# 1388 one-pass products of many widths and operand places, behind the last TensorE operation of a hybrid decoder step

## The chip, the cores and the metric

The kernel runs on one core of a Trainium2 chip, and its time is the device time in microseconds. A profile of one execution gives busy times, waits and the order of the instructions on each engine; its span reaches from the first to the last instruction, and the execution's own time is a little longer.

## The reference, cut to what matters

One inference step of one decoder layer, for a prompt of 256 tokens and 8 single new tokens, 264 columns in all. All data are float32.

```python
def swiglu(x, wg, wu, wd):
    return (jax.nn.silu(x @ wg) * (x @ wu)) @ wd

def trunk_layer(x, attend, shift0, wkv0, lp):
    ...
    x = x + FFN_RES * swiglu(rmsnorm(x, n1), f1g, f1u, f1d)
    h = rmsnorm(x, nm)
    proj = h @ w_in
    ...
    mixed = jnp.concatenate([o_att, o_rwkv.astype(o_att.dtype)], axis=-1)
    x = x + mixed @ w_out
    x = x + FFN_RES * swiglu(rmsnorm(x, n2), f2g, f2u, f2d)
    return x, k_buf, v_buf, S, shift

y_prompt = rmsnorm(xp, final_norm)
y_sample = rmsnorm(xs, final_norm)
```

The model width is 2048 and the FFN width 5504. The attention and the RWKV recurrence between the two FFNs do not touch the change.

## The kernel before, in words

Activations lie transposed: 128 features on the partitions, the 264 tokens as columns. A weight matrix is worked through in blocks of 128 by 128. So that a float32 product can run in TensorE's one-pass format (`F32R` in the code), every operand is split into a rounded part `hi` and the rest `lo`, and three one-pass products stand for one exact product: `hi` with `xh`, `hi` with `xl`, and `lo` with `xh` (`gemm`, lines 136 to 150, through the helper `mm`, line 74). Each call of `mm` on one-pass operands leaves one weight load and one product in the trace; a call on plain float32 operands leaves two of each.

`chunk` (line 125) brings four weight blocks, 512 columns, at a time: SyncE's queue loads `raw`, ScalarE makes `hi`, VectorE makes `lo`. There are four buffers each of `hi` and `lo`. `gemm` sums into a PSUM tile of tag `acc` (three buffers); everything smaller writes tiles of tag `m` (five buffers, `mp`, line 122).

`ffn` (line 227) goes through the 43 FFN blocks in six parts (`PARTS`): the gate and up products of a part, the activation, and then for each of the 16 output blocks `o` the down product of this part, whose result is added to `xr[o]` (line 296). In the last part there are seven blocks, so that each output block has a chunk of four and one of three.

At the end `second_ffn` (line 960) normalises: the sums of squares go through TensorE into `sm`; three products into `hot`, which nobody reads, follow; ScalarE and VectorE make the reciprocal root `rt`; TensorE broadcasts it to all partitions twice, into `rp` for VectorE and into `again`, which ScalarE copies to `rb` for GpSimd. Nine multiplications (lines 998 to 1001) on VectorE and GpSimd scale the stored `ys`, and each is followed by its output DMA on SyncE's or ScalarE's queue. At the start of the kernel `NWARM` = 11 products of `ones` with itself write a tile `warm` that nobody reads either (lines 162 to 164).

A scheduler in the compiler orders each engine's instructions by their place in the program and by when it thinks that their operands are ready; the program states no order by hand around the changed place.

The memory map of the program puts rows of moving operands 1280 bytes apart (`ROW` = 320, line 110) and weight blocks 512 bytes apart.

Of the kernel before, what the change touches and what calls it, by code (L numbers as in the profile page):

```python
# [13 lines left out]
P = 128  # L14
NP = 256
NB = 8
T = NP + NB
# [10 lines left out]
CH, NRAW, NHL = 4, 6, 4  # L28
# [19 lines left out]
def body(tc, I, O):  # L48
    nc = tc.nc
    V, A, G, TE, SP = nc.vector, nc.scalar, nc.gpsimd, nc.tensor, nc.sync  # L50
    cnt = [0]
    big = [None]

    def uid(s):
        cnt[0] += 1
        return f"{s}{cnt[0]}"
# [4 lines left out]
    def stt(out, a, s, b, op0, op1):  # L61
        return V.scalar_tensor_tensor(out=out, in0=a, scalar=s, in1=b, op0=op0, op1=op1)  # L62
# [11 lines left out]
    def mm(out, lhsT, rhs, start=True, stop=True, **k):  # L74
        return TE.matmul(out, lhsT, rhs, start=start, stop=stop, **k)  # L75
# [24 lines left out]
    with ExitStack() as ctx:  # L100
# [21 lines left out]
        def mp():  # L122
            return pp.tile([P, 512], F32, tag="m", bufs=NM, name=uid("m"))
# [12 lines left out]
        def gemm(ps, src, xs, step=None, rng=None, ahead=True, ready=None):  # L136
            n = len(xs)
            for k0 in range(0, n, CH):
                k1 = min(n, k0 + CH)
                if rng and k0 not in rng:  # L140
                    continue
                hi, lo = ready or chunk(src[:, k0 * P:k1 * P], k1 - k0, V, ahead)
                for k in range(k0, k1):
                    xh, xl = xs[k]
                    c = slice((k - k0) * P, (k - k0 + 1) * P)
                    mm(ps[:, :T], hi[:, c], xh, k == 0, False)
                    mm(ps[:, :T], hi[:, c], xl, False, False)
                    big[0] = mm(ps[:, :T], lo[:, c], xh, False, k == n - 1)
                if step:
                    step()  # L150
# [15 lines left out]
        def vc(i):  # L166
            return vec[:, i:i + 1]
# [59 lines left out]
        def ffn(nrm, xr, gu, dn, nxt, load, begin=None, side=None, ready=None):  # L227
            rstd = None
            f0 = 0
            for pi, nf in enumerate(PARTS):  # L230
                hs = hblock(nf)
                late = []
                if begin:
                    early(pi)
                first = pi == 0
                if first:
                    banks = [acc() for _ in range(NACC)] + [mp() for _ in range(NM)]
                    n0 = len(banks) // 2
                    for k in range(len(nrm.xs), CH):
                        at = load(k)  # L240
                    for k0 in range(0, KD, CH):
                        if begin and k0 + CH < KD:
                            begin(k0 // CH + 1)
                        xs = nrm.xs + [None] * (KD - len(nrm.xs))
                        for i, ps in enumerate(banks):
                            with tc.issue_after(at.ins) if begin and k0 == 0 < i else nullcontext():
                                gemm(ps, gu[i // 2, i % 2], xs, rng=(k0,), ahead=False, ready=ready)
                            ready = None
                            if i >= len(banks) - CH and k0 + CH < KD:
                                load(k0 + CH + i - len(banks) + CH)  # L250
                    for f in range(n0):
                        raw = [tmp(), tmp()]
                        V.tensor_copy(raw[0], banks[2 * f][:, :T])
                        A.copy(raw[1], banks[2 * f + 1][:, :T])
                        late.append((f, *raw))
                for f in range(f0 + n0 if first else f0, f0 + nf):
                    pgu = [acc(), acc()]
                    if first and f == n0:
                        sq = iter(range(KD))

                        def step():
                            for k in [x for _, x in zip(range(2), sq)]:
                                nrm.square(xr[k], k % 2, True)
                    else:
                        step = None
                    if begin and pi and copies:
                        copy_one()
                    if side and pi:
                        next(side, None)
                    for ps, w in zip(pgu, (gu[f, 0], gu[f, 1])):  # L270
                        gemm(ps, w, nrm.xs, step)
                    last = f == f0 + nf - 1
                    if rstd is None:
                        rstd = nrm.rstd(tmp())
                    late.append((f, *(x[:, :T] for x in pgu)))
                    now = [late.pop()]
                    for _ in range(len(late) if last else min(len(late), 2 if first and f == n0 + 1 else 1)):
                        now.append(late.pop(0))
                    for j, pg, pu in now:
                        E = V if last else G  # L280
                        g = tmp()
                        tt(V, g, pg, rstd, ALU.mult)
                        s = tmp()
                        act(s, g, AF.Silu)
                        u = tmp()
                        tt(V, u, pu, rstd, ALU.mult)
                        tt(E, u, u, s, ALU.mult)
                        hi, lo = hs[j - f0]
                        A.copy(hi, u)
                        tt(E, lo, u, hi.bitcast(F32), ALU.subtract)  # L290
                if pi == len(PARTS) - 1:
                    nrm.xs = None
                for o in range(KD):
                    ps = acc()
                    gemm(ps, dn[o, :, f0 * P:(f0 + nf) * P], hs)
                    stt(xr[o], ps[:, :T], 0.5, xr[o], ALU.mult, ALU.add)
                    if pi == len(PARTS) - 1:
                        nxt(o)
                f0 += nf

        def first_ffn(n2):
            def load(k0):
# [657 lines left out]
        def second_ffn(n3, xr, XR):  # L960
            fin = Norm(VGF, most=3)

            def load(k):
                if k >= CH:
                    n3.split(xr[k], True)

            with tc.tile_pool(name="f2", bufs=1) as fp:
                cur[0] = (fp, NH)
                ys = [fp.tile([P, 4, T], F32, tag="y", bufs=4, name=uid("y")) for _ in range(4)]
                rt = fp.tile([88, 48], F32, name="rt")  # L970
                sq = fp.tile([P, NQ, T], F32, name="sq")
                n3.sq = fin.sq = [sq[:, j] for j in range(NQ)]

                def nxt(o):
                    fin.square(xr[o])
                    if o == 0:
                        act(rt[:, 7:8], fin.sums[0][0][0:88, 0:1], AF.Sqrt)
                    act(ys[o // 4][:, o % 4], xr[o], AF.Copy, scale=vc(VGF + o))

                side = dec_state(fp, XR)  # L980
                ffn(n3, xr, I["gu2"], I["dn2"], nxt, load, None, side)
                assert next(side, side) is side
                p = fin.sums[0]
                sm, rp, hot = mp(), mp(), mp()
                for i, q in enumerate(p):
                    for j in range(3):
                        mm(sm[0:88, j:j + 1], q[:, j * 88:j * 88 + 88], ones[:, 0:1], i + j == 0, i == 1, skip_group_check=True)
                for _ in range(3):
                    mm(hot[:, :P], ones, p[1][:, :P])
                act(rt[:, 0:3], sm[0:88, 0:3], AF.Sqrt, scale=1.0 / D, bias=eps[0:88, 0:1])  # L990
                V.reciprocal(rt[:, 0:3], rt[:, 0:3])
                for j in range(3):
                    mm(rp[:, j * 88:j * 88 + 88], bc(rt[:, j:j + 1], (88, P)), C[0:88, CID:CID + 88])
                rb, again = tmp(), mp()
                for j in range(3):
                    mm(again[:, j * 88:j * 88 + 88], bc(rt[:, j:j + 1], (88, P)), C[0:88, CID:CID + 88])
                A.copy(rb, again[:, :T])
                for i, (e, o, n) in enumerate(((V, 0, 1), (V, 1, 1), (V, 2, 2), (V, 4, 4), (G, 8, 1), (V, 9, 2), (G, 11, 1), (V, 12, 3), (G, 15, 1))):
                    y = ys[o // 4][:, o % 4:o % 4 + n]
                    r = rb if e is G else rp[:, :T]  # L1000
                    tt(e, y, y, bc(r.unsqueeze(1), (P, n, T)), ALU.mult)
                    (SP, A)[i % 2].dma_start(O["yT"][:, o:o + n, :], y)
# [111 lines left out]
```

## Time and profile before

| what | value |
|---|---|
| median of 2 runs | 1960.09 us (1959.72 to 1960.45) |
| the profiled execution's own time | 1958.83 us |
| its span | 1957.0 us |
| mean granted TensorE clock | 0.998 of full speed |
| PE busy | 1940.1 us, 17011 records |
| PEld busy (weight loads) | 1922.1 us, 17011 records |
| DVE busy | 1313.1 us |
| ACT busy | 1036.4 us |
| POOL busy | 264.1 us |
| HBM | 346.67 MB read, 9.69 MB written |

PE stands for TensorE's products, PEld for its weight loads, DVE for VectorE, ACT for ScalarE, POOL for GpSimd, SP for SyncE; a q behind the name is the engine's sequencer. In lines that group instructions, the shapes stand before the count (x...), then busy time in us and mean duration of one in ns, then the idle time before them. Durations of products overlap, so that the pace of TensorE is read from the starts and not from the durations. In timeline lines the first number is the start in us, the second the time from the first start to the last end of the merged instructions. Since `mm` is one line of code (L75), the products are told apart by their tiles: out<-moving operand,weights.

### The profile page before, as it was taken

To read this page: it belongs to the slowest core of one execution; us is meant where nothing else is said; L and a number is where in the kernel's file an instruction comes from. 1 tells how busy PE (TensorE), PEld (TensorE's weight loads), DVE (VectorE), ACT (ScalarE), POOL (GpSimd) and SP (SyncE) were. 2 spreads that over 40 slices of the span, in tenths; PEclk is the share of its full clock that TensorE was granted. 3 is DMA by queue.
4 is the path that set the end of the run, shared out by engine and by line. 5 is a ranking of instruction groups with operands and counts; after the bars stand their busy time and mean duration, and the time that the engine had idled before them with its cause. 6 is when DMAs were issued, how large, how long until landed. Compare 5 with 4: busy or idle time off the path is not lost.

```text
span 1957.0 us, 45229 instructions
## 1 busy us (share of the span) xinstructions
PE 1940.1 (99%) x17011; PEld 1922.1 (98%) x17011; DVE 1313.1 (67%) x2591; ACT 1036.4 (53%) x2069; POOL 264.1 (13%) x382
## 2 busy tenths in 40 slices
PE   9999999999999999999999999999999999999998
PEld 9999999999999999999889999999999999999998
DVE  5865555655556567799988766766666666666665
ACT  5644444444444456665556755654444444444445
POOL 0401001010010122232210000210101001010012
PEclk9999999999999999999999999999999999999999
DMA  7666666666656567555455455566666666666654
GB/s 241 178 194 194 186 194 196 184 189 178 188 183 185 184 194 230 165 162 153 136 151 167 137 157 185 176 187 188 191 189 193 188 194 191 191 195 183 195 182 148
DMA packets 218875, 357.26 MB, mean 183 GB/s; under 512 B 33552, under 2 KB 72352, under 8 KB 218656
## 3 DMA queue, kind: packets, MB, share of 16 engines
q1 hardware_dynamic: 212144, 345.76, 59.4%
q10 hardware_dynamic: 6512, 8.61, 1.4%
q8 instruction: 133, 2.18, 0.4%
q14 instruction: 86, 0.70, 0.1%
HBM read 346.67 MB, written 9.69 MB: 182 GB/s over the span
## 4 chain that ended last, share of the span: by engine, by line
PE 95%; DVE 3%; DMA 1%; issue 1%; ACT 1%; SPq 0%; DVEq 0%; POOL 0%; ACTq 0%
PE acc L75 87%; PE m L75 7%; DVE lo L59 1%; DVE Xt L59 0%; DVE st L59 0%; DMA Xt<-sa 0%; DMA x<-in_x 0%; DMA raw<-in_win 0%; DVE y L59 0%; SPq L564 0%; DVE gm L59 0%; ACT t L69 0%; DMA sa<-gm 0%; PE m L782 0%; ACT BT L521 0%
## 5 line engine op out<-in xcount | busy, mean ns | idle before, releaser
L59 DVE TENSOR_TENSOR lo<-raw,hi 128x512 fp32r<-128x512 f32 (+1 forms) x1288 | 874.5, 683 | 511.0 <-ACT hi L132 489.8
L132 ACT CAST hi<-raw 128x512 fp32r<-128x512 f32 (+1 forms) x1288 | 777.0, 606 | 822.0 <-PE acc L75 741.5
L75 PE MATMUL acc<-x,hi 128*128 128x264 f32 x5034 | 932.7, 286 | 2.2 <-DVE o L62 1.2
L75 PEld LDWEIGHTS acc<-x,hi 128*128 128x128 f32 x5034 | 781.4, 189 | 5.8 <-ACT hi L132 2.4
L75 PE MATMUL acc<-x,lo 128*128 128x264 f32 x2517 | 719.8, 286 | 0.5 <-DVE lo L59 0.5
L75 PE MATMUL acc<-h,hi 128*128 128x264 f32 x2752 | 495.0, 284 | 0.0
L75 PEld LDWEIGHTS acc<-x,lo 128*128 128x128 f32 x2517 | 475.5, 189 | 2.9 <-DVE lo L59 1.3
L75 PEld LDWEIGHTS acc<-h,hi 128*128 128x128 f32 x2752 | 424.4, 189 | 0.0
L75 PE MATMUL acc<-h,lo 128*128 128x264 f32 x1376 | 387.8, 284 | 0.0
L75 PEld LDWEIGHTS acc<-h,lo 128*128 128x128 f32 x1376 | 259.2, 189 | 0.0
L59 POOL TENSOR_TENSOR t<-t,t 128x264 f32<-128x264 f32 x74 | 80.3, 1085 | 1095.9 <-DVE t L59 949.7
L75 PE MATMUL acc<-y,hi 128*128 128x264 f32 x648 | 122.7, 284 | 0.0
L75 PE MATMUL acc<-o,hi 128*128 128x264 f32 x648 | 120.1, 284 | 0.0
L75 PE MATMUL acc<-kv,hi 128*128 128x264 f32 x582 | 109.2, 284 | 0.0
L75 PEld LDWEIGHTS acc<-y,hi 128*128 128x128 f32 x648 | 101.2, 189 | 0.1
L75 PEld LDWEIGHTS acc<-o,hi 128*128 128x128 f32 x648 | 100.1, 189 | 0.0
L62 DVE SCALAR_TENSOR_TENSOR x<-acc,x 128x264 f32<-128x264 f32 x192 | 81.2, 427 | 24.5 <-PE acc L75 23.6
L75 PE MATMUL acc<-y,lo 128*128 128x264 f32 x324 | 92.0, 284 | 0.0
L75 PE MATMUL acc<-o,lo 128*128 128x264 f32 x324 | 92.0, 284 | 0.0
L75 PEld LDWEIGHTS acc<-kv,hi 128*128 128x128 f32 x582 | 90.0, 189 | 0.0
L59 DVE TENSOR_TENSOR t<-acc,t 128x264 f32<-128x264 f32 x156 | 67.4, 432 | 32.8 <-PE acc L75 32.8
L75 PE MATMUL acc<-kv,lo 128*128 128x264 f32 x291 | 82.7, 284 | 0.0
(280 smaller groups left out, 1534.9 us busy)
## 6 DMA issues: line engine op xcount, KB each, us to landing
raw<-in_gu SPq DMA_DIRECT2D x688, 256.0 KB, 3.4
raw<-in_dn SPq DMA_DIRECT2D x224, 256.0 KB, 2.9
raw<-in_win SPq DMA_DIRECT2D x152, 256.0 KB, 3.4
raw<-in_dn SPq DMA_DIRECT2D x160, 192.0 KB, 2.7
raw<-in_wout SPq DMA_DIRECT2D x64, 256.0 KB, 3.3
xsp<-x ACTq DMA_DIRECT2D x16, 132.0 KB, 3.6
x<-xsp SPq DMA_DIRECT2D x16, 132.0 KB, 4.0
ld<-in_sT SPq DMA_DIRECT2D x16, 128.0 KB, 3.7
```

The lines of the kernel that those rows point to most:

```text
L59: return e.tensor_tensor(out=out, in0=a, in1=b, op=op)
L62: return V.scalar_tensor_tensor(out=out, in0=a, scalar=s, in1=b, op0=op0, op1=op1)
L75: return TE.matmul(out, lhsT, rhs, start=start, stop=stop, **k)
L132: A.copy(hi[:, :w], raw[:, :w])
```

## The change

`gemm` now notes the `hi` and `lo` of the latest chunk of four blocks in a list `wl`, and `ffn` copies that list to `held` after each down product. A new function `wide` is called once, behind the copy of `again` to `rb` and ahead of the nine final multiplications. It allocates one more PSUM tile of tag `m` and multiplies the held `hi` (as weights) with the held `lo` (as moving operand), always into the same tile, each product a group by itself; nobody reads the tile. First come 14 widths of the moving operand, six products each, then 4 widths of the weights, six each, then 256 pairs of starting places, five each: 84 + 24 + 1280 = 1388 products. A step of 4 elements is 16 bytes. All other code stays.

```diff
+    wl = []
...
                 hi, lo = ready or chunk(src[:, k0 * P:k1 * P], k1 - k0, V, ahead)
+                if k1 - k0 == CH:
+                    wl[:] = [hi, lo]
...
                     stt(xr[o], ps[:, :T], 0.5, xr[o], ALU.mult, ALU.add)
+                    held[:] = wl
...
+        held = []
+
+        def wide(w, x):
+            ps = mp()
+            for n in (264, 256, 248, 240, 272, 280, 288, 296, 304, 320, 384, 448, 512, 264):
+                for i in range(6):
+                    mm(ps[:, :n], w[:, 0:P], x[:, 0:n])
+            for m in (32, 64, 96, 128):
+                for i in range(6):
+                    mm(ps[:m, :T], w[:, 0:m], x[:, 0:T])
+            for c in range(0, 64, 4):
+                for d in range(0, 64, 4):
+                    for i in range(5):
+                        mm(ps[:, :T], w[:, c:c + P], x[:, d:d + T])
...
                 A.copy(rb, again[:, :T])
+                wide(*held)
                 for i, (e, o, n) in enumerate(...):
```

## The prediction

> **What bounds the kernel now.** I read the page first: busy shares, the granted clock, the chain that ended last.
>
> ```profile
> span 1957.0 us, 45229 instructions
> PE 1940.1 (99%) x17011; PEld 1922.1 (98%) x17011; DVE 1313.1 (67%) x2591; ACT 1036.4 (53%) x2069; POOL 264.1 (13%) x382
> ...
> PEclk9999999999999999999999999999999999999999
> ...
> PE 95%; DVE 3%; DMA 1%; issue 1%; ACT 1%; SPq 0%; DVEq 0%; POOL 0%; ACTq 0%
> ```
>
> TensorE is the bound: 95% of the chain that ended last is PE, at a clock that the throttle never cut in any slice. So there is no room inside the kernel for 1388 more products; what matters is what one costs and what already stands behind the last of TensorE's work. For the first, the chain over the last stretch, in order of time (start, us, what):
>
> ```profile
> 1929.97 15.13 PE acc L75 x126
> ...
> 1946.13 2.10 PE m L75 x18
> 1948.23 0.02 issue
> 1948.26 0.43 DVE y L59
> 1948.68 0.34 DVEq L1110
> 1949.03 3.28 DVE y L59 x4
> ```
>
> 126 one-pass products of 264 columns take 15.13 us on the chain: 120.1 ns from start to start, with weights loaded anew for each. That pace is the price to carry over. The duration that the groups give is longer, because products overlap in the pipeline:
>
> ```profile
> L75 PE MATMUL acc<-h,hi 128*128 128x264 f32 x2752 | 495.0, 284 | 0.0
> L75 PE MATMUL acc<-y,hi 128*128 128x264 f32 x648 | 122.7, 284 | 0.0
> L75 PE MATMUL acc<-kv,hi 128*128 128x264 f32 x582 | 109.2, 284 | 0.0
> L75 PE MATMUL m<-ones 128*128 128x128 f32 x22 | 4.3, 378 | 1.0 <-POOL eps L159 1.0
> L75 PE MATMUL m<-o,ones 128*128 128x264 f32 x6 | 1.7, 384 | 0.0
> L75 PE MATMUL m<-C,rt 88*128 88x88 f32 x12 | 1.5, 276 | 0.0
> ```
>
> A lone product is in flight for 284 ns, but the next starts after 120; 284 counts once, for the very last. For the second question, the timeline of PE at the end and one stretch of full-precision products for comparison:
>
> ```profile
> 1944.81 0.28 PE L75 MATMUL acc<-h,lo 128*128 128x264 f32 x1
> 1944.93 0.56 PE L75 MATMUL m<-ones,sq 128*88 128x1 f32 x6
> 1946.13 0.63 PE L75 MATMUL m<-ones,sq 128*88 128x1 f32 x6 [0.65 <-ACT sq L69]
> 1946.62 0.91 PE L75 MATMUL m<-sq,ones 128*128 128x128 f32 x6
> 1947.38 1.51 PE L75 MATMUL m<-C,rt 88*128 88x88 f32 x12
> ```
>
> ```profile
> 64.75 1.05 PE L75 MATMUL m<-o,ones 128*128 128x264 f32 x4
> ```
>
> The last weight multiplication of the second FFN starts at 1944.81; then come the sums of squares, the three products on `hot`, and the two broadcasts of the scale (`rp` and `again`, 12 records). PE is through at 1947.38 + 1.51 = 1948.89. A float32 product leaves two records, a one-pass product one. In the run of four float32 records of 264 columns the pace is (1.05 - 0.384) / 3 = 0.222 us a record.
>
> After PE's end 8 us of the span are left: DVE's, ScalarE's and GpSimd's final multiplications, the output DMAs, and the closing drain:
>
> ```profile
> L1110 SPq EVENT_SEMAPHORE  x7: 17/28/3839, 1951.9 to 1957.0; - x7
> L1110 POOLq EVENT_SEMAPHORE  x4: 17/17/17, 1956.4 to 1956.9; - x4
> L1110 PEldq DRAIN  x2: 13/785/1557, 1947.4 to 1956.7; - x2
> ```
>
> SP waits 3.839 us for the outputs' landing; from 1956.4 GpSimd collects the engines, and the span ends at 1957.0. Only these 0.6 us must follow whichever engine is last.
>
> **The change, part by part.** Nothing is removed. The two list assignments run while the program is built and issue no instruction. Keeping `hi` and `lo` of the last four-block chunk alive costs nothing: no later chunk asks for a buffer. The target takes a fifth buffer of tag `m`, beside `sm`, `rp`, `hot` and `again`, and there are five. No product reads what another engine has yet to make, so no wait is added, and no DMA is issued. Products into one bank one after the other are what the 126 of the chain are too.
>
> *Where they begin.* The last record of `m<-C,rt` starts 0.276 before its end, at 1948.61. The pace of that run is (1.51 - 0.276) / 11 = 0.112 us, so the first new product starts near 1948.73. If the compiler's scheduler instead lets a few into PE's wait of 0.65 us for `sq`, the end comes up to 0.65 us sooner; the sum of TensorE's work stays.
>
> *Column part: 84 products.* The fourteen widths add up to 4376, times six 26,256 columns. By 120 ns for 264, 0.4545 ns a column: 11.9 us. Bounds: a constant 120 ns for widths up to 264 and in proportion above gives 12.1; half of the float32 record's 222 ns, 0.4205 ns a column, gives 11.0. The trace has no one-pass product narrower than 264. If the 12 with 240 and 248 columns lost the one-pass price and cost two float32 records (404 and 417 ns), they would add 3.5 us. I take 11.9, since the row of one-pass products is nearest.
>
> *Narrow weights: 24 products of 264 columns with 32, 64, 96 and 128 weight columns.* At 120 ns: 2.9 us. Nearest bounds for the 18 narrow ones: 222 ns a piece adds 1.8 us; below, weights of 32 columns that run beside each other could save at most their 2.2 us. I take 2.9.
>
> *Places: 16 x 16 x 5 = 1280 products of 264 columns.* At 120 ns: 153.6 us. This is the term that decides, and it is the one the trace shows least. In the program's memory map all 14,976 one-pass products of before have the moving operand at byte 96 modulo 256 and the weights at byte 160 modulo 256: one of the 256 combinations that the loops visit. There `y`, `kv` and `h`, tiles far apart, have the same 284 ns a product in the groups. Bounds for another place: below, 112 ns (the pace of `m<-C,rt`, where 88 columns leave only the load of 128 weight columns to bind; half of the float32 record, 111, says the same); above, 222 ns, the pace of a float32 record of the same width, which streams two cycles a column. I take 120 everywhere, as the only row of the same operation.
>
> A rule stands against this price. The Trainium skill, page "TensorE: Matmul & The Clock Gate", section "Back-to-back issue gap", gives columns / 2.4 plus 2.5 ns for a warm stream, 112.5 ns for 264 columns. By it the whole addition would be an estimated 157.9 us in place of 168.4. The trace's 120 ns over 126 products disagrees with it, at a full clock, so the measurement decides.
>
> *Sum.* 11.9 + 2.9 + 153.6 = 168.4 us. The last product ends at 1948.73 + 168.4 - 0.12 + 0.284 = 2117.3. All that followed PE before (final multiplications from 1948.26, output DMAs, SP's wait) now runs beside the new products, which are thirty times as long; were that cover gone, it would cost up to 8 us. Then 0.6 us of closing: span 2117.9. The profiled execution took 1958.83 us, 1.83 more than its span: 2119.7. The median of the two timed runs, 1960.09, lies 1.26 above that execution, so the forecast for the median is 2121.0.
>
> **The rivals.**
>
> *Some places are dear.* If weights and moving operand are read from the same part of memory in the same step, the array waits, and some of the 256 combinations pace slower than 120. For it: 120 ns lies about 8 ns over the two rows that say 111 and 112, so something already holds a one-pass product back, and the trace has only one combination. Against it: the duration is the same to the nanosecond for tiles all over memory. Price: every nanosecond of the mean over places is 1.28 us; one place in five at 222 ns adds 26 us, 2147; a third of them adds 44, 2165; all of them 131, 2252. The Trainium skill says, on the TensorE page named above, section "Part 2: What happens when you issue a matmul", that weights and moving operand come through two independent read ports and loading does not take bandwidth from a running product; by that rule no place would be dear. No trace here shows two places.
>
> *Most places are cheaper.* If the 8 ns over 112 belong to the one combination of before, the 1304 products of 264 columns save 8 ns each, 10.4 us, and the columns up to 0.9: about 2110. For it: the two rows just named. Against it: the pace after the last one-pass product, before a load of only 88 weight columns, is still 1944.93 - 1944.81 = 0.12 us, so the 120 look like the product's own time.
>
> *The products are dropped.* Nobody reads the target, and a compiler may strike out work that nobody reads; then the time stays at 1960, not slower. It decides once fewer than 39 / 0.12 = 327 of the 1388 are left (2% of 1960 is 39 us, about what a measurement of this kernel can tell from no change). Against it: the eleven warm-up products at the start are read by nobody either, and their 22 records stand in the trace (`m<-ones`); so do the six of `hot`.
>
> **How the numbers follow.** Flat at 120 ns, 2121 with 2112 to 2128 as its own range (narrow widths, narrow weights and a nanosecond or two of the places): 0.58. Dear places: 0.27. Cheaper places: 0.12. Dropped: 0.03. The range from 2108 to 2165 takes in the flat case, nearly all of the cheap one and half of the dear one. Slower by over 2%: 0.97, all cases but the last; within 2%: 0.02; faster by over 2%: 0.01, for what I have not seen.
>
> **What would show it.** PE's records rise by 1388 to about 18,400, one for each product; the 1280 stand at starts 0.120 us apart. The chain ends in PE, not in DVE's `y`; the output DMAs have landed near 1956 as before, and the closing after PE's drain takes under 1 us. The granted clock stays full to the end. In the column part the widths show whether pace follows columns or stands at a floor, and whether 240 and 248 jump to 400 ns. I would be wrong if the pace changes from place to place (the place term), if the first new product starts before 1946 or well after 1949, or if the final multiplications wait behind the new products.

## The result, and the profile after

The changed kernel takes 2126.2 us (median of two runs, 2126.15 to 2126.26) against 1960.09: ratio 1.0848, 95% interval 1.0801 to 1.0894. The forecast was 2121.0 within 2108 to 2165. Its profiled execution took 2126.26 us. The kernel before took from 1957.24 to 1962.77 us in sixteen of its seventeen executions beside the second repeat; the seventeenth, at a granted clock of 0.85, took 2101.55 us and is not in the ratios.

The page of the changed kernel, the lines that answer to those shown of before:

```profile
span 2124.5 us, 48006 instructions
PE 2115.4 (100%) x18399; PEld 2096.5 (99%) x18399; DVE 1313.9 (62%) x2591; ACT 1037.0 (49%) x2069; POOL 264.4 (12%) x382
...
PEclk9999999999999999999999999999999999999999
...
PE 97%; DVE 1%; DMA 1%; ACT 1%; issue 0%; SPq 0%; POOL 0%; ACTq 0%; DVEq 0%
...
L76 PE MATMUL m<-lo,hi 128*128 128x264 f32 (+4 forms) x1388 | 170.6, 285 | 0.0
```

PE has 1388 records more, one for each product, and 1388 weight loads more; the counts of DVE, ACT and POOL are those of before. PE's busy time grew by 175.3 us, of which the products are 170.6. PEclk has a 9 in all 40 slices, and over 1949.5 to 2124 the mean granted clock is 1.00. The timeline of PE around the place where they begin, then the chain of that end and the closing drain's lines:

```profile
1949.26 0.56 PE L76 MATMUL m<-ones,sq 128*88 128x1 f32 x6
1950.46 0.63 PE L76 MATMUL m<-ones,sq 128*88 128x1 f32 x6 [0.65 <-ACT sq L70]
1950.95 0.91 PE L76 MATMUL m<-sq,ones 128*128 128x128 f32 x6
1951.70 1.51 PE L76 MATMUL m<-C,rt 88*128 88x88 f32 x12
1953.00 37.17 PE L76 MATMUL m<-lo,hi 128*128 128x264 f32 x289
```

```profile
1950.46 173.11 PE m L76 x1412
```

```profile
L1130 SPq EVENT_SEMAPHORE  x8: 17/28/161247, 1956.3 to 2124.4; - x8
L1130 POOLq EVENT_SEMAPHORE  x4: 17/17/17, 2123.8 to 2124.4; - x4
```

None of the products slipped into PE's wait of 0.65 us for `sq`. The chain runs in PE to 1950.46 + 173.11 = 2123.57; SyncE's closing semaphore waits 161.2 us for PE where it waited 3.8 us for outputs before, and 0.9 us later the span ends. But the sums of squares begin at 1949.26 where they began at 1944.93: 4.33 us are lost ahead of the change, in instructions that the change does not touch.

### The profile page after: what moved, and what is told of

The parts are those of the page before. It is cut to its first block, busy times and chain, and to the rows that moved or that the text cites. A ratio compares the mean times of both kernels' runs of the same rounds, so it can differ in the third digit from the quotient of the medians.

```text
span 2124.5 us, 48006 instructions
## 1 busy us (share of the span) xinstructions
PE 2115.4 (100%) x18399; PEld 2096.5 (99%) x18399; DVE 1313.9 (62%) x2591; ACT 1037.0 (49%) x2069; POOL 264.4 (12%) x382
## 4 chain that ended last, share of the span: by engine, by line
PE 97%; DVE 1%; DMA 1%; ACT 1%; issue 0%; SPq 0%; POOL 0%; ACTq 0%; DVEq 0%
PE acc L76 81%; PE m L76 16%; DVE lo L60 0%; DMA ld<-in_sT 0%; DMA xsp<-x 0%; DMA Xt<-sa 0%; DMA x<-in_x 0%; ACT hi L133 0%; PE m L535 0%; ACT t L70 0%; PE m L801 0%; DVE st L60 0%; PE m L802 0%; PE m L803 0%; DVE Xt L60 0%
## 5 line engine op out<-in xcount | busy, mean ns | idle before, releaser
L76 PE MATMUL m<-lo,hi 128*128 128x264 f32 (+4 forms) x1388 | 170.6, 285 | 0.0
L76 PEld LDWEIGHTS m<-lo,hi 128*128 128x128 f32 (+1 forms) x1388 | 169.9, 187 | 0.5
L76 PE MATMUL acc<-o,hi 128*128 128x264 f32 x648 | 120.1, 284 | 0.0
```

## The experiments

All but the two repeats of the changed kernel put other products in the place of `wide`'s, or move the call. Beside that only the lists differ: `held` also keeps the activation tile `h`, and in the run on pairs `wl` also keeps the chunk before. The product stretches write only the tile that nobody reads. The pace is read as (time of a row less the last product's 0.284 us) / (its count less 1).

**One place, another tile, one group.** The places' pace in the changed kernel, early and late in the place loops:

```profile
1968.15 22.01 PE L76 MATMUL m<-lo,hi 128*128 128x264 f32 x180
...
2099.78 20.40 PE L76 MATMUL m<-lo,hi 128*128 128x264 f32 x167
```

That is 121.4 and 121.2 ns, not 120, and single gaps scatter from 115 to 133 ns, where the down products keep 120. Three kernels of 1280 products asked why:

```diff
-            for n in (264, ...): ...  # all three loops
+            for i in range(1280):
+                mm(ps[:, :T], w[:, 0:P], x[:, 0:T])
```

> Only the 1280 products of the place loops are left, all at the first place (c = d = 0); the 84 and 24 others are gone. Theory A (the place does not matter; a product of 264 columns costs 121.4 ns wherever it starts): mean pace 121.4 ns, 155.4 us for all, the same scatter from 115 to 133 ns. Rival B (the mean of 121.4 hides places that differ): a steady pace of one value, 120 or 122 ns, without scatter. Rival C (instruction supply sets the scatter, since it repeats every 170 products): 121.4 with the same period of 170. For the part ahead of the products, which is the program of before to the instruction: 4.3 us longer than in the profile of before if the added code behind it makes it longer, anywhere from 0 to 4.5 us if it is the scatter between executions.

```diff
+                mm(ps[:, :T], w[:, 0:P], hs[0][0])      # a row of tile h
```

> As the run with one place, but the moving operand is the rounded part of an activation block of the second FFN (tile h), as in the down products, in place of the held lo, which lies right behind the held hi in memory. Theory B' (the 1.4 ns over 120 come from both operands lying in one neighbourhood): 120.0 ns without scatter, 153.6 us for all. Theory C (instruction supply): 121.4 ns as before. Theory D (each product opens a group of its own): 121.4 ns.

```diff
+                mm(ps[:, :T], w[:, 0:P], x[:, 0:T], i == 0, i == 1279)
```

> As the run with one place, but the 1280 products form one accumulation group: only the first starts it, only the last ends it. Theory D (opening a group in each product costs the 1.4 ns): 120.0 ns without scatter. Theories B' and C: 121.4 ns with scatter.

PE's timeline, one line from each in that order:

```profile
1948.46 155.55 PE L76 MATMUL m<-lo,hi 128*128 128x264 f32 x1280
```

```profile
1947.85 153.85 PE L76 MATMUL m<-h,hi 128*128 128x264 f32 x1280
```

```profile
1950.84 155.56 PE L76 MATMUL m<-lo,hi 128*128 128x264 f32 x1280
```

One place: 121.4 ns, with scatter, so theory A's number held, though a single place scatters as much as 256. The other tile: 120.1, and 1275 of its 1279 gaps are 120 to the nanosecond. One group: 121.4. So neither instruction supply (C) nor opening a group (D) costs the 1.4 ns; exchanging the moving operand alone took it away. The times were 2106.69, 2104.37 and 2109.09 us.

**Which pairs.** Theory B' said: operands close together. Eleven pairs, 128 products each:

```diff
+            for a, b in ((w, x[:, 0:T]), (w, h0), (x, h0), (h0, x[:, 0:T]), (h0, h6), (h0, g0),
+                         (x, w[:, 0:T]), (w, w[:, P:P + T]), (x, x[:, P:P + T]), (w, xo[:, 0:T]), (w, wo[:, 0:T])):
+                for i in range(128):
+                    mm(ps[:, :T], a[:, 0:P], b)
```

> Eleven pairs of weights and moving operand, 128 products of 264 columns each, in place of the 1388: (hi, lo), (hi, h0), (lo, h0), (h0, lo), (h0, h6), (h0, g0), (lo, hi), (hi, hi one block on), (lo, lo one block on), (hi, older lo), (hi, older hi); h0, h6 and g0 are rows of the activation tile h of the second FFN, far from hi and lo. Theory B' (the scatter and the 1.4 ns come when both operands lie in one neighbourhood): 121.4 ns with scatter for every pair inside hi and lo and inside h, 120.0 without scatter for (hi, h0), (lo, h0), (h0, lo). Rival E (it comes from lo as the moving operand): 121.4 for (hi, lo), (h0, lo), (lo, lo), (hi, older lo), 120.0 for the rest. The ranges of the part ahead of the products: 1944 to 1949.3 us until the last down product's end, as in the runs so far.

The timeline of PE; the two pairs inside `h` stand merged in one row of 256:

```profile
1951.88 15.78 PE L76 MATMUL m<-lo,hi 128*128 128x264 f32 x128
...
1982.89 15.53 PE L76 MATMUL m<-h,lo 128*128 128x264 f32 x128
1998.26 15.52 PE L76 MATMUL m<-lo,h 128*128 128x264 f32 x128
2013.62 31.23 PE L76 MATMUL m<-h 128*128 128x264 f32 x256
2044.68 15.70 PE L76 MATMUL m<-hi,lo 128*128 128x264 f32 x128
```

(`h0`, `h6` and `g0` are rows of the activation tile `h`.) Pairs between `h` and the weight tiles take 120.0 (`h` as weights with `lo` as moving operand too, so rival E fell); pairs inside one group of tiles, `h` with itself included, 121.4. All as B' had it. But each of the slow pairs also has both operands at the same byte modulo 256, and the fast ones 64 bytes apart. So B' was not yet told from the rival that the distance of the starts decides.

**Which distances.** Here the weights' start moves under each of two moving operands, 128 products a stretch:

```diff
+            for b in (hs[0][0], x[:, 0:T]):
+                for c in range(0, 64, 8):
+                    for i in range(128):
+                        mm(ps[:, :T], w[:, c:c + P], b)
```

> Sixteen stretches of 128 products in place of the 1388: the moving operand is h0 (byte 96 modulo 256) and then lo (byte 160), and under each the weights start 0, 8, 16, ... 56 columns into the held hi (bytes 160, 192, 224, 0, 32, 64, 96, 128 modulo 256). Theory N (the 1.4 ns come when both operands lie in one neighbourhood of memory): 120.0 ns in all eight stretches with h0, 121.4 in all eight with lo. Rival R (they come from the distance of the two starts modulo 256, zero in every pair that showed them so far): with h0, 121.4 ns where the weights start 48 columns in and 120.0 where the distance is not zero; with lo, 121.4 at 0 columns in and 120.0 at 16 and at 48, where the distance is 64 bytes either way.

Four stretches of PE's timeline, cut inside their bounds: `h0` with the weights 16 columns in (distance, moving start less weights' start, 128 modulo 256) and 24 in (96), then `lo` with 32 in (128) and 40 in (96):

```profile
1981.56 15.71 PE L76 MATMUL m<-h,hi 128*128 128x264 f32 x126
1997.35 15.38 PE L76 MATMUL m<-h,hi 128*128 128x264 f32 x125
2136.74 15.34 PE L76 MATMUL m<-lo,hi 128*128 128x264 f32 x123
2152.65 15.13 PE L76 MATMUL m<-lo,hi 128*128 128x264 f32 x123
```

123.4 and 121.7 ns with `h0`, 123.4 and 121.7 with `lo`. The neighbourhood theory fell as it was put: far operands run over 120, near ones at 120.0 (`lo`, weights 8 in). The rival's rule fell as well, for the slow distances are not zero alone. In this run the pace goes with the distance: at 32, 64, 96, 128, 160, 192 and 224 bytes the two moving operands agree to 0.3 ns (122.1, 121.0, 121.7, 123.4, 121.7, 120, 120.0), where of the first `h0` stretch (distance 192) only the second half counts, since the granted clock was 0.50 from 1948.75 to 1952.15. Only at distance 0 do they differ, 120.0 and 121.3; there near and far still tell them apart, as in the run on pairs. Both operands went through the distances in the same falling order, so that a stretch and the one before it changed together.

**All sixteen steps.**

```diff
+            for c in [0] + list(range(0, 64, 4)):
+                for i in range(96):
+                    mm(ps[:, :T], w[:, c:c + P], hs[0][0])
```

> Seventeen stretches of 96 products in place of the 1388, the moving operand h0 throughout: one to bring the clock up, then the weights 0, 4, 8, ... 60 columns into hi, all sixteen steps of 16 bytes. Theory S (the steady pace is a function of the distance of the two starts modulo 256, between 120 and 123.4 ns, and the place loops, with five products a place, show only its mean): the eight even steps repeat the run before to 0.1 ns (120.0, 121.7, 123.4, 121.7, 121.0, 122.1, 120.0, 120.0), none of the odd ones lies under 120.0, and the mean over the sixteen is 121.4, as in the changed kernel. Rival T (the differences come from the order of the stretches, not from the distance): other values at the same steps. Rival U (an odd multiple of 16 bytes costs on its own): the odd steps over 125.

PE's timeline inside the stretches of distance 192, 160, 128 and 96:

```profile
1960.55 11.57 PE L76 MATMUL m<-h,hi 128*128 128x264 f32 x95
1983.60 11.72 PE L76 MATMUL m<-h,hi 128*128 128x264 f32 x95
2006.80 11.44 PE L76 MATMUL m<-h,hi 128*128 128x264 f32 x94
2030.24 11.69 PE L76 MATMUL m<-h,hi 128*128 128x264 f32 x91
```

120.1, 121.7, 120.0 and 126.7 ns. Six of the eight even steps repeat to 0.1 ns; 128 and 96 do not (123.4 and 121.7 before), though both runs take the same rows with the same starts there. The odd steps lie from 120.0 to 123.3, so rival U fell. Nothing lies under 120 by more than 0.05, and the mean over the sixteen is 121.3. So theory S held for the floor and failed at two steps. That the mean agrees with the changed kernel tells little, for one place alone gave 121.4 too. The starts do not fix one pace: at two of them the stream settled into another pattern. Between the two runs the stretch before differs there (distance 160 or 144 ahead of 128, 128 or 112 ahead of 96), and so does the length of the stretches; the order is rival T's part. Nor does the distance hold for other tiles: 64 bytes gave 120.0 with `h0` as weights and `lo` as moving operand in the run on pairs, and 121.0 here and in the run before. No run tells what decides, and the mechanism stays open.

**Widths and the load of the weights.**

```diff
+            for m in (128, 64, 32):
+                for n in (32, 64, 96, 128, 160, 192, 208, 224, 240, 248, 256, 264):
+                    for i in range(24):
+                        mm(ps[:m, :n], w[:, 0:m], hs[0][0][:, 0:n])
```

> In place of the 1388: twelve widths of the moving operand from 32 to 264 columns with 128, 64 and 32 weight columns, 24 products each, the moving operand from h. Theory F (pace is the larger of columns / 2.2 and the load of the weights, which is 112 ns for 128 columns and 0.84 ns a column): with 128 weight columns 112 ns up to 240 and 113 and 120 at 248 and 264; with 64 weight columns 58 ns up to 128 columns, then columns / 2.2; with 32 columns near 32 ns for the narrowest. Rival G (narrow products lose the one-pass price): twice or four times that, 400 ns, below 256 columns. Rival H (weights of fewer columns cost the same load): 112 ns as the floor for all three.

From starts in the trace, means of 22 or more gaps: with 128 weight columns 112 ns for 32 columns, 112 for 208 to 240, 113, 118 and 120 for 248, 256 and 264; with 64 weight columns 58 up to 96 columns, 60 at 128, 89 at 192, 120 at 264; with 32 weight columns 32 at 32 columns, 60 at 128, 120 at 264. That is theory F to within 3 ns; G and H fell. One thing was in nobody's expectation: with 128 weight columns, the later part of the 64 columns, all of 96, 128 and 160, and most of 192 ran at 213 ns. The stretches by windows (bounds, length, PE and PEld busy, then the other engines, granted clock, DMA share and GB/s) show why:

```profile
1949.00:1954.00 5.00, 5.00 (x48) 5.00 (x46) 4.05 (x6) 0.38 (x1) 2.15 (x3) 1.00 0.56 200
1955.00:1975.00 20.00, 20.00 (x95) 20.00 (x95) 0.00 (x0) 0.00 (x0) 0.00 (x0) 0.50 0.11 40
1976.00:2042.00 66.00, 65.84 (x723) 64.99 (x721) 0.00 (x0) 0.00 (x0) 0.00 (x0) 1.00 0.01 1
```

The clock was halved. The gaps go from 112 to 213 ns inside the stretch of 64 columns, at 1954.8, and from 213 back to 112 inside that of 192, at 1975.3. So at full clock both widths keep the floor of 112; 96, 128 and 160 columns with 128 weight columns were not seen at full clock. Why the clock was cut is not shown: this is one execution, and one order of the widths.

**The cover of the tail.** The call moved ahead of the sums of squares:

```diff
+                wide(*held)
                 p = fin.sums[0]
...
-                wide(*held)
```

> All 1388 products as in the changed kernel, but called ahead of the sums of squares, so that the whole tail stands behind them again. My account of the end (8 us of tail hidden beside the products, 0.6 us of closing left): the span from the last down product to the end becomes 170.4 us of products plus 11.2 us (12.07 of before less 0.85 of PE's waits for the squares, which the products cover), 181.6 us, against 175.3 in the changed kernel: some 6 us more. Rival (the closing is not hidden in the changed kernel either, or the tail is hidden here too): the same 175 us.

PE's timeline:

```profile
1948.04 0.28 PE L76 MATMUL acc<-h,lo 128*128 128x264 f32 x1
1948.16 170.48 PE L76 MATMUL m<-lo,hi 128*128 128x264 f32 x1388
2118.47 1.03 PE L76 MATMUL m<-ones,sq 128*88 128x1 f32 x12
```

The span ended at 2129.8, 181.6 us after the products began at 1948.16, against 181.6 expected and 175.2 from the same place in the changed kernel; the time was 2131.55. The tail does lie hidden beside the products in the changed kernel.

**The part ahead of the products.** The changed kernel twice more, and a kernel with one product of the 1388:

> The changed kernel once more, for the part that it shares with the kernel of before. If the 4.3 us by which that part was longer in its first profile are scatter between executions (waits for the transfers of the mixing stage, and the halved clock behind them), the end of the last down product lies anywhere from 1944 to 1949 us and the time over the kernel before is 164 to 168 us by medians; if the added code makes that part longer, it lies at 1949 again and the runs stay 4 us over what the products cost, 2126 us.

> Of the 1388 products one is left; the lists, the held buffers and the fifth tile stay. If the added lines change the part ahead of the products, the time lies above that of the kernel before by the 2 to 4 us seen in the changed kernel; if that part differs only between executions, the ratio is 1.000 with an interval that holds 1.

> The changed kernel once more for the spread of its times beside those of the kernel before. The products and the closing take the same to 0.1 us in each execution; so if the rest is scatter between executions, the lowest times of the two kernels differ by 163.1 us (175.2 us from the last down product to the end, against 12.1), and the two spreads are alike, some 4 us; if the products make the part ahead of them longer, the lowest times differ by 165 us or more.

First repeat: 2123.64 us (2122.75 to 2125.38) against 1958.23, ratio 1.0835, 1.0817 to 1.0853; the difference of 165.4 is inside the 164 to 168 of the scatter. Its profiled execution, the longest of the four, has the sums of squares at 1948.37. One product: ratio 1.0008, 0.9999 to 1.0017. The interval holds 1, but its upper end stands for 3.3 us, so that by itself it does not rule out the 2 to 4 us; and its profile has the sums of squares at 1947.67, 2.7 us later than the kernel before. Second repeat: 2122.37 us (2122.24 to 2123.49) against 1959.79, ratio 1.0832, 1.0818 to 1.0846. Its lowest time is 165.0 over the lowest of before, at the bound that I had set for the rival. But that execution was the profiled one, and its trace tells the two apart (PE's timeline, then windows):

```profile
1943.71 0.56 PE L76 MATMUL m<-ones,sq 128*88 128x1 f32 x6
...
1947.46 172.07 PE L76 MATMUL m<-lo,hi 128*128 128x264 f32 x1388
```

```profile
1947.00:1951.00 4.00, 4.00 (x24) 4.00 (x23) 3.96 (x6) 0.38 (x1) 2.16 (x3) 0.58 0.62 219
```

The sums of squares began at 1943.71, 1.2 us sooner than in the first profile of before: with all 1388 products behind it, that part can be as short as without them. Of the 1.9 us by which 165.0 lies over the expected 163.1, 1.5 are in the products (172.07 against 170.57): the granted clock is 0.58 over the window shown, in which the first of them lie. My expectation that the products take the same to 0.1 us in each execution was wrong.

Where the 4.33 us of the first profile went is told by the windows of the mixing stage, first of before, then of the changed kernel:

```profile
952.00:960.00 8.00, 6.16 (x81) 5.09 (x82) 7.90 (x23) 3.77 (x8) 2.21 (x4) 1.00 0.48 134
...
1016.00:1028.00 12.00, 11.11 (x186) 10.38 (x187) 11.11 (x48) 4.64 (x12) 1.01 (x3) 1.00 0.50 134
1080.00:1092.00 12.00, 12.00 (x113) 11.25 (x112) 6.96 (x30) 7.51 (x24) 0.49 (x2) 1.00 0.48 127
```

```profile
952.00:960.00 8.00, 5.88 (x48) 4.92 (x47) 7.57 (x24) 2.30 (x6) 0.77 (x2) 0.80 0.32 89
...
1016.00:1028.00 12.00, 12.00 (x167) 11.35 (x165) 10.29 (x41) 5.78 (x15) 1.76 (x5) 0.91 0.54 143
1080.00:1092.00 12.00, 12.00 (x115) 11.34 (x114) 7.90 (x31) 6.43 (x21) 0.48 (x2) 0.86 0.43 128
```

In the chain of each, the transfer that reads back the gathered blocks ahead of the first of these windows:

```profile
946.49 4.04 DMA Xt<-sa
```

```profile
947.42 4.65 DMA Xt<-sa
```

In the changed kernel's execution that transfer ended 1.54 us later (952.07 against 950.53). PE's first products behind the waits that both have, each time before and then after, tell what became of it:

```profile
954.55 2.35 PE L75 MATMUL m<-kr,TT 64*64 64x128 f32 x32 [1.46 <-ACT TT L609]
956.09 3.77 PE L76 MATMUL m<-kr,TT 64*64 64x128 f32 x32 [1.45 <-ACT TT L628]
...
995.86 0.48 PE L75 MATMUL acc<-x,hi 128*128 128x264 f32 x2 [1.24 <-DVE o L62]
998.41 0.48 PE L76 MATMUL acc<-x,hi 128*128 128x264 f32 x2 [1.23 <-DVE o L63]
...
1101.28 0.30 PE L701 MATMUL m<-C,XD 128*64 128x128 f32 x1 [0.40 <-ACT XR L703]
1105.63 0.30 PE L720 MATMUL m<-C,XD 128*64 128x128 f32 x1 [0.38 <-ACT XR L722]
```

They are 1.54, 2.55 and 4.35 us apart. So the late transfer accounts for 1.54 us, and the rest was lost between places that enclose the three stretches with a granted clock of 0.50, from 956.83 to 960.22, from 1014.86 to 1018.25 and from 1086.54 to 1089.93; in the profile of before it stayed at 1.00 in all three windows. The first two of these stretches begin behind a wait of PE, of 1.45 and 0.31 us. Ahead of the third PE had waited for nothing since 1055.4, so why the clock was cut there stays open. The first repeat has three such stretches too, the second has none ahead of the products: the same kernel runs either way.

## Why the prediction was right, and where it was off

The time lies inside the range and slower was given 0.97. The mechanism was the one forecast: TensorE is the chain, so its new work is added whole at its pace, and what followed it before is hidden. As differences to the kernel before, 160.9 us were forecast, and 166.1, 165.4 and 162.6 measured. By its steps, the 5.2 us between 2121.0 and 2126.2:

- *Where they begin.* Forecast 1948.73, found 1953.00. From the sums of squares on, 3.80 us were forecast and 3.74 found; the rest, 4.33 us, is the part ahead. This is the step that failed: I took that part's length from one execution, and it differs between executions (what stands behind the last down product began from 1943.7 to 1949.3 in the profiles here). Without that part the forecast is 2.2 us short (163.1 against 160.9). "Well after 1949" was one of my signs for being wrong, and it was so; in the second repeat they began at 1947.46.
- *Column and narrow part.* 14.8 us forecast; the second product of the place loops starts at 1968.15, so it took 15.0. The price by columns was the right one. PE's timeline inside the stretches of 240 and of 512 columns:

```profile
1955.34 0.73 PE L76 MATMUL m<-lo,hi 128*128 128x240 f32 x5
...
1963.27 1.32 PE L76 MATMUL m<-lo,hi 128*128 128x512 f32 x5
```

  With last products of 0.28 and 0.40 us these are 112 and 230 ns: 512 / 2.2 is 233, and 240 stand on the load of 128 weight columns. No width lost the one-pass price, and narrow weights changed nothing at 264 columns.
- *Places.* 120 ns forecast, 121.4 found, 1.8 us more. This term decided the time, and the trace had one combination to price it from; that the other 255 came out close to it was likely by the prediction's chances, not shown, and so in part luck. The rival of dear places was right that places differ and wrong in size: up to 126.7 ns, nowhere near 222. The sentence in the Trainium skill ("TensorE: Matmul & The Clock Gate", "Part 2: What happens when you issue a matmul") by which loading weights takes nothing from a running product left no room for dear places in the prediction, and to this precision there are some: the same products take 120.0 or 123.4 ns as the weights' start moves. No run shows whether the loads are what costs.
- *Cheaper places.* No stretch came under 120. The 8 ns over 112 are the product's own: the pace follows columns / 2.2 from 248 to 512 columns, and loads that bind at 112, 58 and 32 ns do not reach it. The 112.5 ns do not fit this stream, as the prediction held; but the Trainium skill ("TensorE: Matmul & The Clock Gate", "Back-to-back issue gap") calls that formula the gap of an isolated product, so "a warm stream" in the prediction reads it more widely than the section does.
- *The end.* Closing 0.9 us for 0.6; the tail was hidden, which the call ahead of the norm shows. The profile's time lay 0.06 above the median of its runs, where I had added 1.26 to get from a profile to a median; that hid 1.3 us of the misses.
- *Dropped.* All 1388 ran.

Together 4.33 - 0.06 + 2.0 + 0.3 - 0.07 - 1.32 = 5.2 us. The 2.0 are columns and places; the 0.07 are the smaller distance from span to time.

## What to carry to other kernels

Price added TensorE work by start-to-start pace of the same operation at the same operands, not by duration, and add it whole when PE is already the chain; whatever followed PE then becomes free. Before trusting a microsecond, take the part that the change does not touch from several executions: here it scattered by over 5 us, almost three times the error in 1388 products. Where a stream of one-pass products repeats for thousands of records, its pace at the starts in use is worth measuring: from one pair of starts to another it moved by up to 5%, and no rule found here foretells which are slow.

## What the runs showed of the hardware that I had not expected

- One-pass products of 248 to 512 columns pace at about 2.2 columns a nanosecond at full granted clock (120 ns for 264, 230 for 512), and short products stand on the load of their weights at 112, 58 and 32 ns for 128, 64 and 32 columns.
- That pace moves with the starts of the operands, from 120.0 to 126.7 ns with one row as moving operand. At the distance of 192 bytes modulo 256 every stretch of 96 products or more at one pair of starts settled at 120.0; at 96 the same two starts gave 121.7 and 126.7 in two runs, at 128 they gave 123.4 and 120.0. What decides is open.
- The granted clock can fall to 0.50 while PE's records leave no gap: for 20 us under products of 64 to 192 columns with loads of 128 weight columns, in one execution, while with 64 weight columns and 32 to 96 columns it stayed at 1.00; and for 3.4 us in the mixing stage, with no wait of PE in the 30 us before. What the throttle counts as work is open.
